# Instance norm on a DMA-bound core: the first tile in two halves, the last tile loaded ahead of two stores

## The chip, the cores and the metric

The kernel runs on one core of a Trainium2 chip. The metric is the device time of one execution in microseconds (us). Each kernel was run several times, in turn with the kernel before on the same chip. One execution of each kernel left a trace. "The profile" is what that trace says; its span is some 2 us shorter than the device time of the same execution.

## The reference

```python
x = randn(256, 256, 4096), float32          # eps = 1e-5
mean = np.mean(x, axis=2, keepdims=True)
var = np.var(x, axis=2, keepdims=True)
return ((x - mean) / np.sqrt(var + eps)).astype(np.float32)
```

There are 65,536 independent rows of 4096 elements. Every element is read once and written once: 1073.74 MB in and as much out.

## The kernel before

A tile is 128 partitions x 4 rows x 4096 floats, or 8.39 MB, and there are 128 tiles in three buffers. VectorE sums the rows (the "reduces") and scales and shifts three of them in place (the "applies"); ScalarE does the squares, the roots and the apply of the remaining row. All transfers are issued by one engine (SP in the profile) in this order:

```python
def store(s, k, dst):
    take(S, done[s], k)
    S.dma_start(out=dst, in_=X[s][:, :k, :]).then_inc(stored[s], 16)

def load(s, k, src):
    take(S, stored[s], 16)
    S.dma_start(out=X[s][:, :k, :], in_=src).then_inc(loaded[s], 16)
...
load(0, K, x_t[0])
load(1, K, x_t[1])
with S.Fori(0, rounds * BUFS, BUFS) as i:
    for s in range(BUFS):
        store(s, ...)                      # tile i+s
        load((s + 2) % BUFS, ...)          # tile i+s+2
todo = tail[2:]                            # ends with the last tile as two halves, in two buffers
for t, (s, k, _, dst) in enumerate(tail):
    if t == len(tail) - 3:
        load(*todo.pop(0)[:3])             # second half ahead of the last whole store
    store(s, k, dst)
    if todo:
        load(*todo.pop(0)[:3])
```

`take` waits for a semaphore and clears it. The load of tile 2 stands behind the store of tile 0.

## Time and profile before

| What | Before |
|---|---|
| device time, first three runs | 4975.0 to 4977.9 us, median 4976.5 |
| span of the profiled execution | 4973.1 us |
| VectorE (DVE) busy, ScalarE (ACT) busy | 68%, 52% |
| packets of the DMA queue | 99.8% of 16 engines' span |
| first transfer issued, first store issued | 1.27 us, 51.58 us |

The DMA row is the one to read. The lines themselves stand in the prediction below. In the windows view the columns are the stretch in us from the span's start, its length, the busy time (and number of instructions) of DVE, ACT and POOL, the TensorE clock, the DMA share and GB/s. In the timeline they are the start, the duration, the engine, the line, the operation, its operands, a count and, in brackets, the idle time before it.

### The profile page before, as it was taken

How to read it: one execution, taken by the hardware profiler on the slowest of the kernel's cores; microseconds unless marked ns; L12 is line 12 of the kernel's file. 1: busy time of each engine (PE TensorE's matmuls, PEld its weight loads, DVE VectorE, ACT ScalarE, POOL GpSimd, SP SyncE). 2: the span in 40 equal slices, each digit the busy share in tenths (PEclk: the TensorE clock that was granted, in tenths of full speed). 3: DMA queues.
4: the chain of work that ended last, by engine and by line, in shares of the span. 5: the costliest groups of instructions: out<-in, count | busy, mean ns of one | idle time of the engine just before them, and what ended most of it. 6: DMA issues, size and time to landing. Idle time of an engine off the chain costs nothing.

```text
span 4973.1 us, 6421 instructions
## 1 busy us (share of the span) xinstructions
DVE 3396.3 (68%) x2436; ACT 2599.6 (52%) x1493; POOL 0.2 (0%) x4
## 2 busy tenths in 40 slices
DVE  6666666677667776676666776677766766677766
ACT  5455554455545555455545555455554555455545
POOL 0000000000000000000000000000000000000000
DMA  9999999999999999999999999999999999999999
GB/s 380 434 432 432 434 431 434 433 434 434 435 434 434 433 435 434 434 434 433 435 431 438 431 436 433 434 434 433 435 432 436 432 436 431 433 435 432 434 434 411
DMA packets 37155, 2147.52 MB, mean 432 GB/s; under 512 B 4128, under 2 KB 4128, under 8 KB 4128
## 3 DMA queue, kind: packets, MB, share of 16 engines
q1 hardware_dynamic: 37152, 2147.50, 99.8%
q14 instruction: 3, 0.02, 0.0%
HBM read 1073.74 MB, written 1073.74 MB: 432 GB/s over the span
## 4 chain that ended last, share of the span: by engine, by line
DMA 74%; DVE 17%; ACT 7%; issue 1%; another core or an unknown queue 1%; SPq 0%; ACTq 0%; DVEq 0%
DMA x<-in_x_dram 42%; DMA out_dram<-x 32%; DVE part L87 16%; ACT junk L127 3%; ACT x L135 3%; DVE nsum L89 1%; DVE nmean L91 1%; DVE x L107 0%; ACTq L153 0%; SPq L141 0%; ACT std L132 0%; SPq L145 0%; ACTq L69 0%; ACT L119 0%
## 5 line engine op out<-in xcount | busy, mean ns | idle before, releaser
L87 DVE TENSOR_REDUCE part<-x 128x64 f32<-128x4096 f32 x512 | 2258.8, 4412 | 1438.2 <-DMA x<-in_x_dram 1438.2
L127 ACT ACTIVATE junk<-x,nmean 128x4096 f32<-128x4096 f32 x512 | 1882.2, 3676 | 2337.3 <-DVE nmean L91 2337.3
L107 DVE TENSOR_SCALAR x<-x,rstd,nbias 128x4096 f32<-128x4096 f32 x383 | 912.5, 2411 | 37.7 <-DVE nbias L99 16.0
L135 ACT ACTIVATE x<-x,nbias,rstd 128x4096 f32<-128x4096 f32 x129 | 488.5, 3787 | 0.0
L89 DVE TENSOR_REDUCE nsum<-part 128x1 f32<-128x64 f32 x512 | 112.7, 220 | 17.7
L127 ACT ACTIVATION_READ_ACCUMULATOR junk<-x,nmean 128x1 f32 x512 | 95.5, 187 | 0.0
L91 DVE TENSOR_SCALAR nmean<-nsum 128x1 f32<-128x1 f32 x512 | 78.7, 154 | 17.5
L97 DVE RECIPROCAL rstd<-std 128x3 f32<-128x3 f32 (+1 forms) x258 | 42.0, 163 | 39.9 <-ACT std L119 31.5
L127 ACT ACT_TABLE_LOAD x41 | 52.6, 1283 | 2.0 <-DVE eps_tile L177 1.2
L119 ACT ACT_TABLE_LOAD x41 | 52.6, 1283 | 0.7
L99 DVE TENSOR_TENSOR nbias<-nmean,rstd 128x3 f32<-128x3 f32 (+1 forms) x258 | 41.5, 161 | 8.9
L132 ACT ACTIVATE std<-ss,eps_tile 128x1 f32<-128x1 f32 x129 | 38.0, 295 | 15.0
L119 ACT ACTIVATE std<-ss,eps_tile 128x3 f32<-128x3 f32 x129 | 38.2, 296 | 3.3
L177 DVE MEMSET eps_tile<- 128x1 f32 x1 | 0.1, 59 | 1.0 <-SPq L152 1.0
L208 POOL MEMSET const-bfloat16-1.0<- 128x1 bf16 x1 | 0.1, 101 | 0.0
L208 POOL MEMSET const-uint8-127<- 128x1 uint8 x1 | 0.1, 101 | 0.0
L208 POOL MEMSET const-float32-0.0<- 128x1 f32 x1 | 0.1, 98 | 0.2 <-issue 0.2
L208 POOL MEMSET const-float32-1.0<- 128x1 f32 x1 | 0.1, 98 | 0.0
## 6 DMA issues: line engine op xcount, KB each, us to landing
x<-in_x_dram SPq DMA_DIRECT2D x2, 4096.0 KB, 29.6
out_dram<-x SPq DMA_DIRECT2D x2, 4096.0 KB, 17.4
x<-in_x_dram SPq DMA_DIRECT2D x127, 49.1
out_dram<-x SPq DMA_DIRECT2D x127, 30.4
```

Of the source, the lines that this page charges most:

```text
L87: mine(V.tensor_reduce(out=part[s][:, r, :], in_=row, axis=AX.X, op=ALU.add))
L89: mine(V.tensor_reduce(out=nsum[s][:, c], in_=part[s][:, r, :], axis=AX.X, op=ALU.add, negate=True))
L91: V.tensor_scalar_mul(out=nmean[s][:, c], in0=nsum[s][:, c], scalar1=1.0 / d).then_inc(means, 1)
L97: mine(V.reciprocal(out=rstd[s][:, c], in_=std[s][:, c]))
L99: mine(V.tensor_mul(out=nbias[s][:, c], in0=nmean[s][:, c], in1=rstd[s][:, c]))
L107: V.tensor_scalar(out=x[:, r, :], in0=x[:, r, :], scalar1=rstd[s][:, c], scalar2=nbias[s][:, c], op0=ALU.mult, op1=ALU.add,).then_inc(done ...
L119: A.activation(out=std[s][:, : k - 1], in_=ss[s][:, : k - 1], func=AF.Sqrt, bias=eps_tile, scale=1.0 / d).then_inc(stds, 1)
L127: A.activation(out=junk, in_=x[:, r, :], func=AF.Square, bias=nmean[s][:, c], scale=1.0, accum_out=ss[s][:, c]).then_inc(own_a, 1)
L132: A.activation(out=std[s][:, c], in_=ss[s][:, c], func=AF.Sqrt, bias=eps_tile, scale=1.0 / d).then_inc(stds, 1)
L135: A.activation(out=x[:, k - 2, :], in_=x[:, k - 2, :], func=AF.Identity, bias=nbias[s][:, c], scale=rstd[s][:, c]).then_inc(done[s], 1)
L177: V.memset(eps_tile, eps).then_inc(ready, 1)
L208: nc = _bacc.Bacc("TRN2", target_bir_lowering=False, num_devices=1)
```

## The change

The intent is to keep the DMA queue filled at both ends. The first tile is loaded as two halves and each half is stored as soon as it is done, so that a store is there when the first loads run out. The last tile is loaded whole, ahead of the stores of the two tiles before it, and is worked on and stored in halves. The loop keeps its order.

```diff
-                load(0, K, x_t[0])
-                load(1, K, x_t[1])
-                with S.Fori(0, rounds * BUFS, BUFS) as i:
-                    for s in range(BUFS):
-                        store(s, ...)
-                        load((s + 2) % BUFS, ...)
-                ... (tail as above)
+                for h in range(2):
+                    r = half_of(h)
+                    S.dma_start(out=X[0][:, r, :], in_=x_t[0][:, r, :]).then_inc(second(loaded, 0, h), 16)
+                load(1, 1, wait=False)
+                store_half(0, 0, 0)
+                store_half(0, 0, 1)
+                load(2, 2, wait=False)
+                store(1, 1)
+                take(S, stored[BUFS], 16)
+                load(0, 3)
+
+                with S.Fori(0, rounds) as i:
+                    for t in range(L0, L0 + BUFS):
+                        store(t % BUFS, (t, BUFS, rounds, i))
+                        load((t + 2) % BUFS, (t + 2, BUFS, rounds, i))
+                load(last % BUFS, last)
+                store((last - 2) % BUFS, last - 2)
+                store((last - 1) % BUFS, last - 1)
+                store_half(last % BUFS, last, 0)
+                store_half(last % BUFS, last, 1)
...
+                halves(vector_tile, 0, True)        # VectorE; ScalarE likewise
+                vector_tile(1)
...
+                halves(vector_tile, last % BUFS, False)
```

More of the change, by code (lines that the diff above doesn't have):

```diff
@@ L35 @@
     out_t = out_flat.rearrange("(t p k) d -> t p k d", p=P, k=K)
+    assert ntiles == 128
     half = K // 2
-    h0 = n - P * K
-    x_h = x_flat[h0:n, :].rearrange("(h p k) d -> h p k d", p=P, k=half)
-    out_h = out_flat[h0:n, :].rearrange("(h p k) d -> h p k d", p=P, k=half)
     pool = ctx.enter_context(tc.tile_pool(name="pool", bufs=1))
@@ L53 @@
     )
-    loaded = [nc.alloc_semaphore(f"loaded{s}") for s in range(BUFS)]
-    stored = [nc.alloc_semaphore(f"stored{s}") for s in range(BUFS)]
+    loaded = [nc.alloc_semaphore(f"loaded{s}") for s in range(BUFS + 1)]
+    stored = [nc.alloc_semaphore(f"stored{s}") for s in range(BUFS + 1)]
     own_v = nc.alloc_semaphore("own_v")
@@ L63 @@
     scaled = nc.alloc_semaphore("scaled")
-    done = [nc.alloc_semaphore(f"done{s}") for s in range(BUFS)]
+    done = [nc.alloc_semaphore(f"done{s}") for s in range(BUFS + 1)]
     ready = nc.alloc_semaphore("ready")
@@ L71, with vector_tile @@
     V, A, S = nc.vector, nc.scalar, nc.sync
-    def vector_tile(s, k):
+    def vector_tile(s, r0=0, k=K, ld=None, dn=None):
         x = X[s]
+        ld = loaded[s] if ld is None else ld
+        dn = done[s] if dn is None else dn
         own = 0
@@ L81, in mine @@
             return instruction.then_inc(own_v, 1)
-        take(V, loaded[s], 16)
-        for r in range(k):
+        if ld:
+            take(V, ld, 16)
+        for r in range(r0, r0 + k):
             c = slice(r, r + 1)
@@ L91, in vector_tile @@
             V.tensor_scalar_mul(out=nmean[s][:, c], in0=nsum[s][:, c], scalar1=1.0 / d).then_inc(means, 1)
-        for i, c in enumerate((slice(0, k - 1), slice(k - 1, k))):
+        last = r0 + k - 1
+        for i, c in enumerate((slice(r0, last), slice(last, last + 1))):
             if i == 0:
@@ L104, in vector_tile @@
                 take(V, own_v, own)
-            for r in range(0, k - 2) if i == 0 else (k - 1,):
+            for r in range(r0, last - 1) if i == 0 else (last,):
                 c = slice(r, r + 1)
@@ L109, in vector_tile, with scalar_tile @@
                     op0=ALU.mult, op1=ALU.add,
-                ).then_inc(done[s], 1)
-    def scalar_tile(s, k):
+                ).then_inc(dn, 1)
+    def scalar_tile(s, r0=0, k=K, ld=None, dn=None):
         x = X[s]
-        for r in range(k):
+        dn = done[s] if dn is None else dn
+        last = r0 + k - 1
+        for r in range(r0, r0 + k):
             c = slice(r, r + 1)
-            if r == k - 1:
+            if r == last:
                 A.wait_ge(own_a, k - 1)
                 A.activation(
-                    out=std[s][:, : k - 1], in_=ss[s][:, : k - 1], func=AF.Sqrt, bias=eps_tile, scale=1.0 / d
+                    out=std[s][:, r0:last], in_=ss[s][:, r0:last], func=AF.Sqrt, bias=eps_tile, scale=1.0 / d
                 ).then_inc(stds, 1)
@@ L123, in scalar_tile @@
             else:
-                if r:
-                    A.wait_ge(own_a, r)
-                A.wait_ge(means, r + 1)
+                if r > r0:
+                    A.wait_ge(own_a, r - r0)
+                A.wait_ge(means, r - r0 + 1)
             A.activation(
@@ L130, in scalar_tile, with rows_of, store, load @@
         take(A, own_a, k)
-        c = slice(k - 1, k)
+        c = slice(last, last + 1)
         A.activation(out=std[s][:, c], in_=ss[s][:, c], func=AF.Sqrt, bias=eps_tile, scale=1.0 / d).then_inc(stds, 1)
-        c = slice(k - 2, k - 1)
+        c = slice(last - 1, last)
         take(A, scaled, 1)
         A.activation(
-            out=x[:, k - 2, :], in_=x[:, k - 2, :], func=AF.Identity, bias=nbias[s][:, c], scale=rstd[s][:, c]
-        ).then_inc(done[s], 1)
-    def store(s, k, dst):
-        take(S, done[s], k)
-        S.dma_start(out=dst, in_=X[s][:, :k, :]).then_inc(stored[s], 16)
-    def load(s, k, src):
-        take(S, stored[s], 16)
-        S.dma_start(out=X[s][:, :k, :], in_=src).then_inc(loaded[s], 16)
-    rounds = (ntiles - 4) // BUFS
-    tail = [(t % BUFS, K, x_t[t], out_t[t]) for t in range(rounds * BUFS, ntiles - 1)]
-    tail += [((ntiles - 1 + h) % BUFS, half, x_h[h], out_h[h]) for h in range(2)]
+            out=x[:, last - 1, :], in_=x[:, last - 1, :], func=AF.Identity, bias=nbias[s][:, c], scale=rstd[s][:, c]
+        ).then_inc(dn, 1)
+    def rows_of(ap, t):
+        if isinstance(t, int):
+            return ap[t]
+        first, period, count, i = t
+        ap = ap[first : first + period * (count - 1) + 1 : period]
+        return ap[bass.ds(i, 1)].rearrange("o p k d -> p (o k) d")
+    def store(s, t):
+        take(S, done[s], K)
+        S.dma_start(out=rows_of(out_t, t), in_=X[s][:, :, :]).then_inc(stored[s], 16)
+    def load(s, t, wait=True):
+        if wait:
+            take(S, stored[s], 16)
+        S.dma_start(out=X[s][:, :, :], in_=rows_of(x_t, t)).then_inc(loaded[s], 16)
+    def half_of(h):
+        return slice(h * half, (h + 1) * half)
+    def second(sems, s, h):
+        return sems[BUFS] if h else sems[s]
+    def store_half(s, t, h):
+        r = half_of(h)
+        take(S, second(done, s, h), half)
+        S.dma_start(out=out_t[t][:, r, :], in_=X[s][:, r, :]).then_inc(second(stored, s, h), 16)
+    def halves(tile_fn, s, first):
+        for h in range(2):
+            ld = second(loaded, s, h) if first or h == 0 else False
+            tile_fn(s, h * half, half, ld, second(done, s, h))
+    last = ntiles - 1
+    rounds = (ntiles - 5) // BUFS
+    L0 = 2
     with tc.tile_critical():
@@ L156, in _ @@
             def _(sync):
-                for s in range(BUFS):
-                    S.sem_inc(stored[s], 16)
-                load(0, K, x_t[0])
-                load(1, K, x_t[1])
-                with S.Fori(0, rounds * BUFS, BUFS) as i:
-                    for s in range(BUFS):
-                        store(s, K, out_t[bass.ds(i + s, 1)].rearrange("o p k d -> p (o k) d"))
-                        load((s + 2) % BUFS, K, x_t[bass.ds(i + s + 2, 1)].rearrange("o p k d -> p (o k) d"))
-                todo = tail[2:]
-                for t, (s, k, _, dst) in enumerate(tail):
-                    if t == len(tail) - 3:
-                        load(*todo.pop(0)[:3])
-                    store(s, k, dst)
-                    if todo:
-                        load(*todo.pop(0)[:3])
-                for s in range(BUFS):
+                for h in range(2):
+                    r = half_of(h)
+                    S.dma_start(out=X[0][:, r, :], in_=x_t[0][:, r, :]).then_inc(second(loaded, 0, h), 16)
[15 more added lines that the diff above has]
+                store_half(last % BUFS, last, 1)
+                for s in ((last - 2) % BUFS, (last - 1) % BUFS, last % BUFS, BUFS):
                     take(S, stored[s], 16)
@@ L177, in _ @@
                 V.memset(eps_tile, eps).then_inc(ready, 1)
+                halves(vector_tile, 0, True)
+                vector_tile(1)
                 with V.Fori(0, rounds) as i:
-                    for s in range(BUFS):
-                        vector_tile(s, K)
-                for s, k, _, _ in tail:
-                    vector_tile(s, k)
+                    for j in range(BUFS):
+                        vector_tile((L0 + j) % BUFS)
+                vector_tile((last - 2) % BUFS)
+                vector_tile((last - 1) % BUFS)
+                halves(vector_tile, last % BUFS, False)
             @block.scalar
@@ L186, in _ @@
                 take(A, ready, 1)
+                halves(scalar_tile, 0, True)
+                scalar_tile(1)
                 with A.Fori(0, rounds) as i:
-                    for s in range(BUFS):
-                        scalar_tile(s, K)
-                for s, k, _, _ in tail:
-                    scalar_tile(s, k)
+                    for j in range(BUFS):
+                        scalar_tile((L0 + j) % BUFS)
+                scalar_tile((last - 2) % BUFS)
+                scalar_tile((last - 1) % BUFS)
+                halves(scalar_tile, last % BUFS, False)
 _INS = ['x', 'eps']
```

## The prediction

> **What bounds the kernel now.** I began with the page's head, its busy rows and its DMA part:
>
> ```profile
> span 4973.1 us, 6421 instructions
> DVE 3396.3 (68%) x2436; ACT 2599.6 (52%) x1493; POOL 0.2 (0%) x4
> q1 hardware_dynamic: 37152, 2147.50, 99.8%
> HBM read 1073.74 MB, written 1073.74 MB: 432 GB/s over the span
> ```
>
> The compute engines have 32% and 48% of idle time, while the one DMA queue's packets take 99.8% of 16 engines' span. So bytes set the time, and only stretches in which the DMA engines have nothing to do can be won by a change that moves the same bytes. A tile is 128 x 4 x 4096 x 4 = 8.39 MB, and the input and output are 2 x 128 tiles. I then asked for busy time by stretch (start:end us, length, DVE, ACT, POOL, clock, DMA share, GB/s). I chose the borders so that they fall on the edges of the idle stretches:
>
> ```profile
> 0.00:2.27 2.27, 0.06 (x1) 1.02 (x1) 0.20 (x4) 1.00 0.00 0
> 2.27:41.85 39.58, 18.33 (x10) 11.89 (x8) 0.00 (x0) 1.00 0.99 424
> 41.85:52.40 10.55, 9.35 (x11) 9.04 (x6) 0.00 (x0) 1.00 0.00 0
> 52.40:91.10 38.70, 25.36 (x19) 19.49 (x11) 0.00 (x0) 1.00 1.06 434
> 1000.00:1116.00 116.00, 79.70 (x58) 60.99 (x36) 0.00 (x0) 1.00 1.00 434
> 4956.00:4959.40 3.40, 1.22 (x1) 1.87 (x1) 0.00 (x0) 1.00 0.70 299
> 4969.10:4973.09 3.99, 0.00 (x0) 0.00 (x0) 0.00 (x0) 1.00 0.02 8
> ```
>
> In the steady part the queue is full: 1.00 at 434 GB/s, so a transfer of one tile takes 8.39 MB / 434 GB/s = 19.3 us, and a tile's load and store take 38.7 us. There are four idle stretches: 2.27 us before the first packet, 10.55 us from 41.85 on, in 4956.0 to 4959.4 a partial one of 0.30 x 3.4 = 1.0 us, and some 4 us of emptying and ending. The timeline tells what made the second:
>
> ```profile
> 1.27 0.86 SPq L145 DMA_DIRECT2D x<-in_x_dram  x2
> 23.32 4.42 DVE L87 TENSOR_REDUCE part<-x 128x64 f32<-128x4096 f32 x1 [22.23 <-DMA x<-in_x_dram]
> 48.92 2.41 DVE L107 TENSOR_SCALAR x<-x,rstd,nbias 128x4096 f32<-128x4096 f32 x1
> 51.58 0.36 SPq L141 DMA_DIRECT2D out_dram<-x  x1
> 52.20 0.35 SPq L145 DMA_DIRECT2D x<-in_x_dram  x1
> ```
>
> Two loads are queued at 1.27; the first lands at 23.23 and the second ends at 41.85. Nothing further is queued until the first store at 51.58, because the load of tile 2 stands behind it in program order. Tile 0 takes 28.3 us of work (23.3 to 51.6) against the 18.6 us of loading left at 23.3. That is the gap. At the end the same view gives:
>
> ```profile
> 4921.47 36.82 SPq L141 DMA_DIRECT2D out_dram<-x  x3
> 4923.30 4.42 DVE L87 TENSOR_REDUCE part<-x 128x64 f32<-128x4096 f32 x1 [1.95 <-DMA x<-in_x_dram]
> 4940.22 4.41 DVE L87 TENSOR_REDUCE part<-x 128x64 f32<-128x4096 f32 x1
> 4954.08 3.79 ACT L135 ACTIVATE x<-x,nbias,rstd 128x4096 f32<-128x4096 f32 x1
> ```
>
> The last tile is already halved there: the first half waits 1.95 us for its load, and the last store is issued at 4921.47 + 36.82 - 0.35 = about 4957.95, just after some engines ran dry.
>
> **What the Trainium skill says.** "DMA: Bandwidth & Descriptors", section Specifications, gives a fabric ceiling of 435 GB/s and a share of about 358 GB/s of HBM for a core. The trace agrees with the first (434 in the steady stretch) and not with the second for this single core, so I take 434 as a hard ceiling for loads and stores together. The same page, section "Anatomy of one DMA", has a fixed part of about 2.0 us per transfer, mostly the receipt after the last byte. The trace shows about the same at the start: issue at 1.27, first packets at 2.27, landing at 23.23, so 21.96 - 19.3 = 2.7 us. It is seen only where the queue runs empty; behind other transfers it is hidden. "ScalarE: Activation LUTs", section "What ACT_TABLE_LOAD costs", has 1283 ns for a table load; the page before has 1283 ns as well, 82 times.
>
> **The change, part by part.**
>
> First tile. The two half loads stand ahead of the load of tile 1. A half is 9.7 us of transfer, so the first should land at 1.0 + 2.7 + 9.7 = 13.4 instead of 23.2 (the three semaphore increments ahead of the first load, 0.23 us in the chain, go as well). For the work on a half I take the durations of the halved last tile before: start to store issue is 4940.22 to 4957.95, or 17.7 us, and the second half's reduce starts 4940.22 - 4923.30 = 16.9 us after the first's. In the first half a table load of 1.28 us now lies ahead of the first root, between the two squares; about 0.5 us of that falls into a wait of ACT for the second mean (0.73 us before 4933.05), so it costs some 0.8 us. So the first half's store is issued at 13.4 + 17.7 + 0.8 = 31.9, the second half starts at 13.4 + 16.9 + 0.8 = 31.1, and its store is issued at 48.8. The loads keep the DMA busy to 41.8 as before, then the first half's store covers 41.8 to 51.5, and the second half's store with the load of tile 2 behind it has packets ready at 48.8 + 1.0 = 49.8. This is 1.7 us before the queue would run dry, so the gap closes completely. Next, tile 1 starts at about 48.0 and needs 27.4 us (51.25 to 78.67 before), so its store is issued at 75.4, while the queue holds work until 51.5 + 9.7 + 19.3 = 80.5. Tile 2 lands there, is done 28 us later at 109, and the queue then holds work until 80.5 + 38.7 = 119. That is the steady slack of before, 10.7 us. Won: 10.55 us, plus some 0.2 us of earlier start. The added costs are one more issue on SP (0.35 us, with a full queue behind it) and half transfers in place of whole ones, hidden by a full queue.
>
> Last tile. Its load comes at the place in the queue where the store of tile 125 was, so it lands one transfer earlier, at about 4913 in the old clock rather than 4923 and 4933, and the 1.95 us wait of DVE goes: tile 127 starts when tile 126 leaves DVE, at 4921.35, and its last store is issued at 4956.0 rather than 4957.95. The queue is in the same order of bytes from there on, and ends with the same half store. The partial gap of 1.0 us should shrink to about 0.2 us, so 0.8 us are won. The landing of the last store is unchanged: the end costs what it did.
>
> The loop. Same bytes, same order, same three buffers. The order of instructions on ACT shows that the two table loads now stand only in the first half tile and no longer in the loop: 80 x 1.28 = 103 us of ACT busy time go, all beside DMA-bound time, so worth nothing.
>
> Sum: 4976.5 - 10.55 - 0.2 - 0.8 = **4965 us**, a quarter of a per cent.
>
> **The rivals.**
>
> 1. The gap moves instead of closing. If a half takes over 1.7 us longer than I worked out (a later landing, a costlier table load), the DMA engines run dry for the difference around 51 us. For it: the slack is small and worked out from the other end of the run. Against it: it costs only the excess, so with 2 us more the gap is 0.3 us; even without any overlap of half and table load it would stay near 1 us. Time 4966 to 4967.
>
> 2. The first tile's loads and stores in halves, now taken from rows of a tile that are not contiguous across partitions (32 KB out of each 64 KB), run slower, or stores beside loads do. For it: just after the gap, 50 to 100 us, the page's row by slices shows only 380 GB/s in the first slice of 124 us, and not all of that is the two idle stretches (12.8 of 124 us at 434 would leave 389). Against it: only four transfers of 4.2 MB are of this kind; if they were 20% slower, it would cost 4 x 9.7 x 0.2 = 8 us. The halved tile at the end before ran at about 434. I give this a tenth; time 4970 to 4973.
>
> 3. The steady rate depends on how loads and stores lie against each other, and the change shifts that phase. The slices vary between 431 and 438 GB/s, and 1 GB/s over the whole span is 4973 / 434 = 11 us. For it: the early slices are a little slower than the middle ones (432 against 434), some 6 us in all by my reading. Against it: the order of transfers and the slack of 10.7 us are unchanged in the loop. It could go either way by 3 us.
>
> 4. The load queued early at the end delays the two stores behind it and so the end. Against it: the bytes are the same and the queue is full, so the order can't matter unless the last store is later. It is not. Time as predicted.
>
> **Range and chances.** The three runs of before span 2.9 us, so 1.5 us either way is noise. With 3 us for the phase (rival 3) and up to 5 us upwards for rivals 1 and 2, I take 4960 to 4971. Two per cent is 99.5 us; all idle DMA time together is below 18 us, so faster by 2% is nearly excluded. For slower by 2%, the loop itself would need to lose 0.8 us per tile, and it has 10.7 us of slack. I give each 0.01.
>
> **What would show it.** Right: DMA share near 1.00 in 42 to 52 us; half stores issued near 32 and 49; the load of tile 2 near 49.4; the span shorter by 11 to 12 us; no wait of DVE for a load ahead of tile 127; 2 table loads instead of 82 with no effect. Wrong in step one: an idle stretch of over 1 us near 50. Wrong by rival 3: mid-run slices of another rate than 434. The prediction is wrong as a whole if the gap is closed and the time isn't some 11 us shorter.

## The result, and the profile after

Ratios here are the mean time of one kernel's fast runs over that of the other's of the same rounds, so they are not quite the ratios of the medians that are quoted.

| | Before | Changed |
|---|---|---|
| runs | 6 | 6 |
| lowest, median, highest us | 4975.0, 4975.7, 4977.9 | 4961.9, 4963.6, 4968.4 |
| profiled span us | 4973.1 | 4960.3 |

The ratio is 0.9976, with a 95% interval of 0.9963 to 0.9989: the same within 2%, and 12.1 us less by the medians. The head of the changed kernel's page and its DMA part:

```profile
span 4960.3 us, 6348 instructions
DVE 3390.1 (68%) x2439; ACT 2505.6 (51%) x1416; POOL 0.2 (0%) x4
q1 hardware_dynamic: 37296, 2147.50, 100.0%
HBM read 1073.74 MB, written 1073.74 MB: 433 GB/s over the span
```

The bytes are the same and the queue's share has gone from 99.8% to 100.0%. ScalarE lost 94 us of busy time with 80 table loads of 1.28 us gone (and one more apply of 3.8 us done), and the span shows no trace of so large an amount. Busy time by stretch:

```profile
1.98:41.50 39.52, 22.18 (x19) 18.86 (x13) 0.00 (x0) 1.00 1.03 424
41.85:52.40 10.55, 7.52 (x7) 6.28 (x5) 0.00 (x0) 1.00 0.93 401
52.40:91.10 38.70, 30.17 (x20) 23.14 (x13) 0.00 (x0) 1.00 1.01 436
1000.00:1116.00 116.00, 79.67 (x58) 58.61 (x34) 0.00 (x0) 1.00 1.00 434
4940.50:4944.00 3.50, 1.96 (x1) 2.60 (x1) 0.00 (x0) 1.00 0.56 243
```

The second line is the stretch in which the DMA share was 0.00 before. It is 0.93 now and not 1.00 because this view puts a packet's whole time where the packet starts; the packet records behind it show no engine idle there. The steady stretch has the same 434 GB/s as before. The last line is the dip near the end: the mean DMA share was 0.70 for 3.4 us before and is 0.56 for 3.5 us now. The timeline of SP at both ends:

```profile
0.96 0.86 SPq L188 DMA_DIRECT2D x<-in_x_dram  x2
1.88 0.42 SPq L159 DMA_DIRECT2D x<-in_x_dram  x1
31.38 17.24 SPq L170 DMA_DIRECT2D out_dram<-x  x2
48.67 0.45 SPq L159 DMA_DIRECT2D x<-in_x_dram  x1
74.72 0.33 SPq L154 DMA_DIRECT2D out_dram<-x  x1
...
4870.02 39.09 SPq L154 DMA_DIRECT2D out_dram<-x  x2
4926.27 17.24 SPq L170 DMA_DIRECT2D out_dram<-x  x2
```

The half stores of the first tile are issued at 31.38 and 31.38 + 17.24 - 0.35 = 48.3 us (predicted 31.9 and 48.8), the load of tile 2 at 48.67. The last store is issued at 4926.27 + 17.24 - 0.35 = 4943.2 us, after the dip in DMA share had begun.

So the start went as intended. Two things were not plain from this pair. Does the tail earn anything? And is the gain dependable?

### The profile page after: what moved, and what is told of

It reads as the page before. It is cut to its first block, busy times and chain, and to the rows that moved or that the text cites. A ratio compares the mean times of both kernels' runs of the same rounds, so it can differ in the third digit from the quotient of the medians.

```text
span 4960.3 us, 6348 instructions
## 1 busy us (share of the span) xinstructions
DVE 3390.1 (68%) x2439; ACT 2505.6 (51%) x1416; POOL 0.2 (0%) x4
## 4 chain that ended last, share of the span: by engine, by line
DMA 71%; DVE 19%; ACT 7%; another core or an unknown queue 1%; issue 1%; SPq 0%; ACTq 0%; DVEq 0%
DMA x<-in_x_dram 40%; DMA out_dram<-x 31%; DVE part L89 17%; ACT junk L132 3%; ACT x L140 3%; DVE nsum L91 1%; DVE x L110 1%; DVE nmean L93 1%; ACTq L182 0%; ACT std L137 0%; DVE nbias L102 0%; SPq L159 0%; SPq L154 0%; DVE rstd L100 0%
## 5 line engine op out<-in xcount | busy, mean ns | idle before, releaser
L100 DVE RECIPROCAL rstd<-std 128x1 f32<-128x1 f32 (+1 forms) x260 | 41.7, 160 | 17.2 <-ACT std L137 16.5
L102 DVE TENSOR_TENSOR nbias<-nmean,rstd 128x1 f32<-128x1 f32 (+1 forms) x260 | 41.6, 160 | 8.9
L137 ACT ACTIVATE std<-ss,eps_tile 128x1 f32<-128x1 f32 x130 | 38.3, 295 | 15.1
L124 ACT ACTIVATE std<-ss,eps_tile 128x3 f32<-128x3 f32 (+1 forms) x130 | 38.5, 296 | 4.2
L132 ACT ACT_TABLE_LOAD x1 | 1.3, 1283 | 1.2 <-DVE eps_tile L211 1.2
L124 ACT ACT_TABLE_LOAD x1 | 1.3, 1283 | 0.0
```

Of the source, the lines that this page charges most:

```text
L100: mine(V.reciprocal(out=rstd[s][:, c], in_=std[s][:, c]))
L102: mine(V.tensor_mul(out=nbias[s][:, c], in0=nmean[s][:, c], in1=rstd[s][:, c]))
L124: A.activation(out=std[s][:, r0:last], in_=ss[s][:, r0:last], func=AF.Sqrt, bias=eps_tile, scale=1.0 / d).then_inc(stds, 1)
L132: A.activation(out=junk, in_=x[:, r, :], func=AF.Square, bias=nmean[s][:, c], scale=1.0, accum_out=ss[s][:, c]).then_inc(own_a, 1)
L137: A.activation(out=std[s][:, c], in_=ss[s][:, c], func=AF.Sqrt, bias=eps_tile, scale=1.0 / d).then_inc(stds, 1)
```

## The experiments

**Theory A**, the prediction's: the gap at the start is worth 10.75 us and the tail 0.8 us, because idle engine time costs its mean over the 16 DMA engines (the later expectations call it the mean-gap theory). **Theory B**: at the end only the last of the 16 DMA engines counts. If that one never runs dry, the tail is worth nothing (the slowest-engine theory). **Theory C**: the tail, or ScalarE's table loads, make a good part of the 12 us.

Twelve kernels were run. Those of one set shared a chip and the runs of the kernel before. All gave correct results.

| Set | Kernel | All runs, us | Kernel before, median |
|---|---|---|---|
| 1 | changed, again | 4963.6 4997.4 4963.9 5009.7 4963.4 4999.4 | 4975.3 (11 runs) |
| 1 | start only | 4963.4 4964.2 5001.4 4963.7 4964.0 5006.9 | |
| 1 | tail only | 4973.4 4973.8 4974.2 4976.0 4973.9 | |
| 1 | three loads | 4963.5 4967.9 4967.5 4963.5 5006.0 4962.3 | |
| 2 | first store delayed by 3 reduces | 4976.7 4976.0 4976.8 4974.8 4976.4 | 4976.1 (9 runs) |
| 2 | first store delayed by 1 reduce | 4965.4 4967.0 4965.7 4967.4 4966.4 | |
| 2 | last store delayed by 1 reduce | 4963.1 4963.2 4964.6 4964.6 4963.1 | |
| 2 | whole last tile | 4963.7 4963.9 4962.1 4963.2 4963.4 | |
| 3 | changed, third time | 4965.9 4963.2 4963.8 4965.4 4965.0 | 4975.7 (11 runs) |
| 3 | warm tables | 4973.8 4974.9 4974.0 4974.5 4974.7 | |
| 3 | last store delayed by 3 reduces | 4971.1 4973.7 4971.9 4977.2 5015.8 4970.9 | |
| 3 | three loads, whole last tile | 4963.0 5012.7 4969.7 4963.8 5006.3 4971.1 | |

Nine runs stand near 5000 us, the lowest at 4997.4; all others lie below 4979. All are labelled fast, at a granted clock of 1.0, as they are less than 1.5% above the fastest. I call them the **second mode**, take "good" runs to be those below 4990, and come back to them after the single experiments.

The next table is counted from the packet records of each trace, which carry a start and a duration for every packet. A packet of 65,536 bytes takes 2.418 us at its usual pace. Columns: the time of all packets above that pace, as a mean over 16 DMA engines; the mean idle time of an engine between 40 and 66 us; how many of the 16 stood idle for over 0.4 us after 4900 us, and the mean of that idle time over all 16; when the first and the last of them finished. The records do not name the engine, so packets were chained by their times.

```
kernel                  slow packets  idle 40-66   dry at the end   first end   last end
before                      9.0          10.67     11, mean  1.08     4968.5     4971.2
changed                     5.7           0.00      8, mean  1.45     4953.8     4958.5
changed, again              6.0           0.00     10, mean  1.95     4954.9     4959.6
changed, third time         7.7           0.00      9, mean  2.27     4956.5     4962.0
start only                  6.7           0.00     13, mean  2.36     4956.6     4959.6
tail only                   6.7          10.44      7, mean  1.26     4965.1     4969.8
three loads                 5.8           0.00     10, mean  2.30     4954.7     4959.8
first delayed, 3           10.6           9.53      6, mean  1.01     4968.1     4972.8
first delayed, 1            7.9           0.65      7, mean  1.51     4957.1     4961.8
last delayed, 1             5.9           0.00     14, mean  4.53     4958.2     4959.1
last delayed, 3             5.7           0.00     16, mean 13.75     4967.1     4967.3
whole last tile             6.0           0.00     15, mean  4.30     4958.0     4960.0
three loads, whole last     5.4           0.00     15, mean  3.85     4957.0     4959.3
warm tables                 9.1           9.82      8, mean  0.94     4967.5     4970.2
```

### 1. The changed kernel, again

No edit.

> The changed kernel itself, once more, as the yardstick for the three beside it. Both theories: 4962 to 4967 us, 10 to 13 us under the kernel before of the same rounds. In its profile no idle DMA stretch near 42 to 52 us.

Good runs: 4963.4 to 4963.9, or 11.8 us under before by the means. But three of six took 4997 to 5010 us, which neither theory expected, and the ratio over all runs is 1.0023 (0.9994 to 1.0051). The gain of the first measurement doesn't show on this chip when all runs are counted.

### 2. The start alone

```diff
# changed kernel, with the tail of before
-                load(last % BUFS, last)
                 store((last - 2) % BUFS, last - 2)
+                ... load first half of the last tile, load second half into the next buffer
                 store((last - 1) % BUFS, last - 1)
-                store_half(last % BUFS, last, 0)
-                store_half(last % BUFS, last, 1)
+                ... store first half, store second half
```

> The halved first tile with the tail of before. Theory A (the start gap is worth 10.75 us and the reordered tail 0.8 us, as I predicted): 10.75 us under before, 0.8 us over the changed kernel. Theory B (the DMA engine that ends last never ran dry in either tail, so the tail is worth nothing): the same time as the changed kernel within its own scatter of some 2 us. Theory C (the tail makes a good part of the 12 us): 3 us or more over the changed kernel. The rounds can tell C from the others, hardly A from B.

The good runs, 4963.4 to 4964.2, match the changed kernel's of the same set (4963.4 to 4963.9). Theory C falls as far as the tail goes: with the old tail the whole gain is there. The table loads have left the loop here too, so what they are worth is told by experiments 3 and 10 and not by this one. The 0.8 us of theory A are too few to tell from nothing here. Two of six runs were in the second mode, so that mode doesn't need the new tail.

### 3. The tail alone

```diff
# changed kernel, with a whole first tile and the order of before
-                (two half loads of tile 0)
+                load(0, 0, wait=False)
                 load(1, 1, wait=False)
-                store_half(0, 0, 0)
-                store_half(0, 0, 1)
+                store(0, 0)
                 load(2, 2, wait=False)
                 store(1, 1)
-                take(S, stored[BUFS], 16)
                 load(0, 3)
```

> The start of before with the reordered tail; the table loads leave the loop here as well. Theory A: 0.8 us under before. Theory B: before within 1 us. Theory C: 3 us or more under before. The idle stretch of 10.5 us near 42 to 52 us must be there again in all three.

The mean is 1.15 us under before. The first load is issued at 0.96 instead of 1.27, which is 0.3 of it. The rest, 0.85 us, would fit theory A's 0.8, but the scatter of single runs is 2.6 us in this kernel and 2.9 us in before, so this run alone settles nothing. The idle stretch is back, 10.44 us by the packet records, and with it nearly all of the time. As the page of this kernel has only 2 table loads, their absence from the loop is worth no more than these 1.15 us.

### 4. Three whole loads first

```diff
# on the kernel of experiment 3
                 load(1, 1, wait=False)
+                load(2, 2, wait=False)
                 store(0, 0)
-                load(2, 2, wait=False)
                 store(1, 1)
```

> The changed kernel with a whole first tile, but the load of tile 2 queued ahead of the store of tile 0, as its buffer is free. If the gap is only a lack of queued transfers (theories A and B): three loads keep the DMA busy until 2.3 + 3 x 19.3 = 60.3 us, the store comes at 51.6 us, no idle stretch, time as the changed kernel within 2 us. If halving itself is what helps (shorter transfers, earlier first landing): about 10 us over the changed kernel, that is near before.

Three whole loads and a first store as late as in before. The timeline of SP:

```profile
0.96 1.34 SPq L159 DMA_DIRECT2D x<-in_x_dram  x3
51.08 27.43 SPq L154 DMA_DIRECT2D out_dram<-x  x2
```

The first store is issued at 51.08 (51.58 before), yet no engine was idle between 40 and 66 us. Three of six runs took 4962.3 to 4963.5, two 4967.5 and 4967.9, and one was in the second mode. Halving is not what closes the gap: moving one line, so that a third load is queued while its buffer is free anyway, fills the same hole. The two runs near 4967.7 and one in the second mode make it no better than the changed kernel.

### 5. The first store delayed by three reduces

```diff
# changed kernel; in the second half of tile 0, ahead of the last apply, on VectorE
+                for _ in range(3):
+                    V.wait_ge(own_v, own)
+                    row = x[:, last, :].rearrange("p (c f) -> p c f", c=C)
+                    mine(V.tensor_reduce(out=part[s][:, last, :], in_=row, axis=AX.X, op=ALU.add))
                 take(V, own_v, own)
```

> The changed kernel with three useless reduces ahead of the last apply of the first tile's second half: its store comes some 12.6 us later (3 x 4.43 less 0.7 that ScalarE was behind anyway), against about 2 us of slack, so an idle DMA stretch of about 10.5 us near 51 us is back. Gap theory: 4973 to 4976 us, as before, one for one. The runs of the yardstick have shown a second mode (4997 to 5010 us in 6 of 18 runs of the three kernels without the gap, in none of 16 with it). If the gap, by making all DMA engines start again together, keeps a kernel out of that mode: none of these six runs above 4980. If the mode comes with the new order or the halves or the chip: about two of six near 5000.

The timeline of SP, then the windows of this kernel around the place:

```profile
31.42 29.95 SPq L174 DMA_DIRECT2D out_dram<-x  x2
61.42 0.43 SPq L163 DMA_DIRECT2D x<-in_x_dram  x1
```

```profile
42.40:52.00 9.60, 7.23 (x4) 5.71 (x4) 0.00 (x0) 1.00 1.01 437
52.40:62.10 9.70, 9.52 (x4) 0.00 (x0) 0.00 (x0) 1.00 0.13 54
```

The second half's store is 12.7 us later (29.95 against 17.24 in the changed kernel), the DMA engines are idle for a mean of 9.5 us, and the time is that of before: 4976.4 by the median against 4963.2 and 4963.4 for the two kernels without a delay there in this set. The dose went in at the start and came out at the end. It came out a little large: 13 us of time for 9.5 us of idle. The slow packets, 10.6 us against 5.9 and 6.0, account for it in size, and what makes packets slower is not explained. In the other three kernels with such a stretch they were 6.7 to 9.1 us. No run was in the second mode, but no kernel of this set had one, so the question whether the gap keeps it away stays open.

### 6. The first store delayed by one reduce

The same edit with `range(1)`.

> The same with one useless reduce: the store comes 3.7 us later, so a short idle stretch of about 1.7 us. Gap theory: 1.7 us over the changed kernel, some 4965 us. If any stretch in which all DMA engines stand keeps the second mode away: no run above 4980, and this would be the best kernel. If it takes a long one, or if the gap has nothing to do with it: about two of six near 5000.

The time is 4966.4, or 3.1 us over the two kernels without a delay in this set, where 1.7 were expected. The store came 3.8 us later (21.05 against 17.24), but only 0.65 us of idle time came of it, as the slack was 3 us rather than 2. By the packet records the engines ran dry at 52.4 us, and the store issued at 31.48 + 21.05 - 0.35 = 52.2 had its first packets at 53.1. By idle time alone it should have cost under 1 us; slow packets are 7.9 us against 5.9, so the remainder is again of that kind. A miss in size, and no answer on the second mode for the same reason as above.

### 7. The last store delayed by one reduce

The same edit in the second half of the last tile, with `range(1)`.

> The changed kernel with one useless reduce ahead of the last apply of the last tile's second half: the last store is issued 3.7 us later. Mean-gap theory (idle engine time at the end costs its mean, on which my 0.8 us for the tail rested): its good runs are 3.7 us longer, some 4967 us. Slowest-engine theory (the DMA engine that ends last still has some 5 us of the store before it to move when the last store is issued, so only the engines that are ahead run dry): good runs unchanged, 4962 to 4964 us. Second mode, no gap at the start: about two of six near 5000.

This is the experiment that tells A from B. The timeline of SP, then the window of the dip in the changed kernel and in this one:

```profile
4926.86 21.06 SPq L174 DMA_DIRECT2D out_dram<-x  x2
```

```profile
4938.00:4948.00 10.00, 2.73 (x3) 4.99 (x4) 0.00 (x0) 1.00 0.88 380
4938.00:4948.00 10.00, 7.16 (x4) 5.58 (x4) 0.00 (x0) 1.00 0.52 226
```

The last store is issued at 4926.86 + 21.06 - 0.35 = 4947.6, which is 3.8 us later from the store before it than in the changed kernel. In the ten microseconds around it the mean DMA share is 0.52 (0.88 in the same window of the changed kernel). By the packet records 14 of 16 engines ran dry, for a mean of 4.5 us. The one that never did is the one that ended last. And the time is 4963.2, where theory A said 4967. (The changed kernel itself was not in this set: its good runs elsewhere have medians of 4963.6 to 4965.0, and the kernel of experiment 8, beside this one, has 4963.4.) Theory A falls for the tail: at the end, idle engine time did not cost its mean. The engines finish between 4958.2 and 4959.1 instead of between 4953.8 and 4958.5, so those that were ahead only waited. In the gap at the start, by contrast, no engine had work left: in before each of the 16 stood idle there for 10.3 to 11.0 us.

### 8. The last tile whole

```diff
# changed kernel
-                store_half(last % BUFS, last, 0)
-                store_half(last % BUFS, last, 1)
+                store(last % BUFS, last)
```

> The changed kernel with a whole last tile: its one store is issued some 6 us earlier than the second half's was, before any DMA engine runs dry. Mean-gap theory: the 1.5 us mean of idle engine time at the end of the changed kernel goes, 1 to 1.5 us under it. Slowest-engine theory: unchanged within 1 us. Second mode: if it has to do with the tail, none near 5000; if not, about two of six.

4963.4, unchanged, as theory B has it. One part of my expectation was wrong: the one store is issued at 4937.7, earlier than the second half's was, but with no first half's store to fill the time 15 engines ran dry all the same, for a mean of 4.3 us. That makes the verdict stronger. Neither the halves nor the 5.5 us by which the last store came earlier mattered to the time; experiment 11 shows how late it may come.

### 9. The changed kernel, a third time

No edit.

> The changed kernel a third time, for the second mode: near 5000 us it stood in 3 of 6 runs on one chip and in none of 6 in its first measurement; two kernels with the same start had none in 10 runs on another chip. If the mode is of the chip: all six alike here, either about half near 5000 or none. If it is a chance of the kernel wherever it runs: about two of six. Good runs 4962 to 4967.

4963.2 to 4965.9, and no second mode, while two kernels beside it on the same chip had it in three of twelve runs. So a chip does not have the mode in all of its runs or in none. That fits a chance in each run, and five runs are too few to be sure of meeting what came in 3 of 17; it is not shown.

### 10. Warm tables

```diff
# kernel before, ScalarE ahead of its loop
                 take(A, ready, 1)
+                A.activation(out=std[0][:, 0:1], in_=eps_tile, func=AF.Sqrt, bias=eps_tile, scale=1.0).then_inc(own_a, 1)
+                take(A, own_a, 1)
```

> The kernel before with one root taken on a small tile ahead of ScalarE's loop, so that the 82 table loads become 1 and some 104 us of ScalarE busy time go, as in the changed kernel, while transfers and their order stay those of before. My prediction: worth nothing but the loads of the first tile, which lie in the gap: the 1.28 us load ahead of the first root delays the first store by up to 1 us, so 0 to 1 us under before. Rival (part of the 12 us comes from ScalarE's table loads): 3 us or more under before.

The group rows of table loads in the kernel before, then that of this kernel and its row of busy times, and the timeline of SP at its first store:

```profile
L127 ACT ACT_TABLE_LOAD x41 | 52.6, 1283 | 2.0 <-DVE eps_tile L177 1.2
L119 ACT ACT_TABLE_LOAD x41 | 52.6, 1283 | 0.7
```

```profile
L187 ACT ACT_TABLE_LOAD x1 | 1.3, 1283 | 1.2 <-DVE eps_tile L177 1.2
DVE 3392.1 (68%) x2436; ACT 2500.4 (50%) x1413; POOL 0.2 (0%) x4
```

```profile
50.60 0.37 SPq L141 DMA_DIRECT2D out_dram<-x  x1
```

One table load instead of 82, and 99 us less busy time on ScalarE. The first store is 0.98 us earlier (50.60 against 51.58), because one of those loads lay ahead of the first root, in the gap. The idle stretch is shorter by 0.85 us. The runs are 1.5 us under before by the means and 1.1 by the medians. At most 1 was expected. The gap accounts for 0.85 us, and what is left is within the scatter of the runs (3.8 us in before), so the other 80 loads show no worth.

### 11. The last store delayed by three reduces

The edit of experiment 7 with `range(3)`.

> Three useless reduces ahead of the last apply: the last store comes 12.6 us later. One of them cost nothing, though most DMA engines stood idle for up to 7 us. Slowest-engine theory: the engine that ends last had some 5 us left, so 12.6 - 5 = 7 to 9 us over the changed kernel, about 4971, and all engines end together. Mean-gap theory: 12.6 us over. If the end has nothing to do with the last store: unchanged.

The window of this kernel around the last store, and its span:

```profile
4938.00:4948.00 10.00, 7.73 (x4) 5.61 (x4) 0.00 (x0) 1.00 0.49 210
4948.00:4961.00 13.00, 8.27 (x3) 0.00 (x0) 0.00 (x0) 1.00 0.29 124
...
span 4969.0 us, 6351 instructions
```

The good runs have a median of 4971.9 against 4965.0 for the changed kernel in this set, so 6.9 us (8.3 by the means), where theory B said 7 to 9 and theory A 12.6. Now every one of the 16 engines ran dry, for a mean of 13.75 us and the least of them for 7.9, and they finish together, between 4967.1 and 4967.3. The store came 12.7 us later (29.97 against 17.24), so the last engine had some 5 us of slack: the delay of 3.8 us cost nothing, and this one cost what was above the slack.

### 12. Three loads first, last tile whole

The edits of experiments 3, 4 and 8 together: no halves anywhere.

> No halves at all: three whole loads queued first, whole last tile loaded ahead of two stores. If halving is worth nothing at either end beyond keeping the queue filled: the time of the changed kernel within 1 us, 4962 to 4965, with a simpler kernel. If the two ends add something together: 1 to 2 us less. Second mode as for the changed kernel beside it.

The two best runs are 4963.0 and 4963.8 and the profiled span, 4961.2, is that of the changed kernel. Two more are at 4969.7 and 4971.1 and two in the second mode, so "within 1 us" held for half of the good runs only. In the two kernels that open with three whole loads, 4 of 9 good runs lie between 4967.5 and 4971.1; in those that open with two halves and have no such delay as in experiments 5, 6 and 11, 1 of 28 does (4968.4). I made this grouping after seeing the runs, and its cause is open; but it speaks against calling the halves worthless. No experiment made a version that beats the changed kernel. With a whole last tile the changed kernel (experiment 8) has the same time with simpler code.

### The second mode

| | Runs | Above 4990 us |
|---|---|---|
| no idle stretch at the start (changed three times, start only, three loads, last delayed twice, whole last, three loads and whole last) | 51 | 9 |
| a stretch of 10 us (before 37, tail only, first delayed by 3, warm tables) | 52 | 0 |
| a stretch of 0.65 us (first delayed by 1) | 5 | 0 |

If both kinds had the same chance, all nine would fall on the first with a probability of C(51,9)/C(103,9) = 0.0012. But I formed the grouping on seeing set 1, where it was 6 of 18 against 0 of 16. In sets 2 and 3 alone it was 3 of 27 against 0 of 30, and that would happen by chance with C(27,3)/C(57,3) = 0.10. Set 2 had none in any kernel. And 37 of the 52 runs are of the one kernel before, which has other table loads and another tail as well: without it, it is 9 of 51 against 0 of 15, which would happen by chance with C(51,9)/C(66,9) = 0.08. So the association is likely and not proved, and the chip or the hour may play a part too. Neither the new tail nor the halves are needed: start only had it in 2 of 6 runs, three loads in 1 of 6.

Its cause is open. All traces are of first executions and none was in the second mode, so no packet of it has been seen. An extra of 34 to 50 us over a span of 4960 us would be 0.7 to 1.0% on all packets, or one long stop; the runs don't tell which. What matters is the average. All 17 runs of the changed kernel have a mean of 4970.9 us, its 14 good runs one of 4964.2. Against a mean of 4975.9 for the 37 runs of before, the change earned 11.7 us in good runs and 5.0 us on the average of all.

## Why the prediction was right or wrong

The predicted range, 4960 to 4971, held the measured 4963.6, and "same within 2%" was right. That the sum, 4965, came so near is in part luck: its 0.8 us for the tail were not there, and some 3 us fewer of slow packets, which it did not foresee, came in the same direction. By its steps:

- **DMA bound, steady part unchanged.** Right: 434 GB/s in the same stretch of both kernels.
- **The gap closes, 10.55 us.** Right, and shown three ways. The idle time goes from 10.67 us to nothing in the packet records; the start alone carries the whole gain (experiment 2); the gap put back takes it away (experiment 5). The mechanism is a lack of queued transfers and not the halving (experiment 4).
- **Its slack of 1.7 us.** Too small. It was worked out from a first half landing at 13.4, a store at 48.8 and a queue that runs dry at 51.5; they were at 13.1, 48.3 and (with the store delayed) 52.4. A delay of 3.8 us made only 0.65 us of idle time, so the slack was about 3 us.
- **0.2 us of an earlier start.** Right, and slightly more: first issue at 0.96 instead of 1.27.
- **The tail, 0.8 us.** This step failed. The prediction said: "The partial gap of 1.0 us should shrink to about 0.2 us, so 0.8 us are won." The partial gap did not shrink; it is 1.45 us on the mean of the engines in the profiled changed kernel. And it would not have mattered, as experiments 7 and 8 show: the 16 engines are up to 5 us apart by then, the dip is made by those that are ahead, and the last one still has work. The 1.95 us wait of VectorE did go, and the last store was issued 2 us earlier, as worked out (17.1 us before the end of the span against 15.1); it bought nothing.
- **The table loads are worth nothing.** Right for 80 of them. The one load ahead of the first root in the gap was worth about 1 us in before (experiment 10). In the changed kernel that load is still there, hidden by the slack.
- **Rival 1** (the gap moves) did not happen. **Rival 2** (half transfers are slow) did not either. **Rival 4** (the early load at the end does harm) found nothing for it.
- **Rival 3** (phase) was right in kind and too small by far. I gave 3 us either way. Slow packets changed by about 3 us, from 9.0 to 5.7, in the profiled pair. That is the second largest item of its 12.8 us, although the last engine decides and so the items don't simply add. But the second mode, which nothing in the profile of before announced, costs 34 to 50 us when it comes. Through it 3 of 17 runs of the changed kernel fell outside the range.

## What to carry to other kernels

In a kernel that is bound by its DMA queue, look for the stretches with nothing queued, ask which free buffer could already have a load, and expect about the idle time back (here 10.7 us of it gave 12.1, and 9.5 put back cost 13, with slow packets the likely rest); the 94 us of busy time taken off ScalarE bought nothing that could be seen. Near the end, read the DMA share per engine and not as a mean: a dip to a half cost nothing here while one engine still had work. And a gain of a quarter of a per cent needs many runs on several chips: here a slow mode that the kernel before never showed took back more than half of it on the average.

## What the Trainium skill lacked or had wrong

- "DMA: Bandwidth & Descriptors", section "Where 436 GB/s comes from", says that for transfers between HBM and SBUF the HBM side, about 358 GB/s, binds. On this single core loads and stores together ran at 434 GB/s for the whole steady part. "HBM Reference", section "Specifications (TRN2)", does say that a core streaming alone measures well above its share.
- "Perfetto Trace Analysis", section "What "DMA-bound" means", names specific DMA engines as a possible bound, but no page that I read has a figure for how far the engines of one queue stand apart at the end of a steady stream, or says what idle time of those that are ahead costs there. Here they finished up to 4.7 us apart (4953.8 to 4958.5), a mean of 4.5 us of idle engine time cost nothing, and a delay of 3.8 us of the last store was free.
- No page that I read tells of a second mode on one core without a change of clock: 9 of 51 runs without an idle stretch at the start were 34 to 50 us longer at a granted clock of 1.0, against 0 of 52 with one.
- "ScalarE: Activation LUTs", section "What ACT_TABLE_LOAD costs", adds a drain of about 1380 ns to each load of 1283 ns. The load had its 1283 ns here, but no such drain is seen: in the changed kernel the load starts at 21.89 us and the root that needs it at 23.18, which is 1.29 us later; the instruction before the load ended at 21.88.
